# Two of four weight-block sums per feature made by accumulating transfers, and a fast product scheme rewritten with one half's rows negated

## The chip, the cores and the metric

The kernel runs on one core of a Trainium2 chip. The metric is the device time of one launch in microseconds (us), lower is better. A core has five engines that run their own instruction streams in order: TensorE (PE in the profile; its weight loads are shown apart as PEld), VectorE (DVE), ScalarE (ACT), GpSimd (POOL) and SyncE (SP). SP only issues transfers here; a transfer that SP, ACT or POOL has issued is carried out by sixteen DMA engines while the issuing engine goes on. An instruction that waits for a transfer or for another engine holds up everything behind it on its own engine.

## The reference

One layer of a hybrid encoder trunk is applied to a prompt of 2048 tokens and to a sample of 8 x 16 tokens, with model width 1024. Chunk-band attention and an mLSTM run side by side and are mixed by an out-projection. A gated convolutional feed-forward network (FFN) follows, and the change lies there:

```python
def conv_ffn(h, buf, w_up, w_conv, b_conv, w_down):
    u = h @ w_up                                   # 1024 -> 2 * 2816: gate rows, up rows
    ext = jnp.concatenate([buf.astype(u.dtype), u], axis=1)
    y = b_conv
    for j in range(CONV_W):                        # causal depthwise convolution, width 3
        y = y + ext[:, j:j + S] * w_conv[j]
    gate, up = jnp.split(y, 2, axis=-1)
    out = (jax.nn.gelu(gate, approximate=True) * up) @ w_down
    return out, ext[:, S:]
...
x = x + rms_norm(mix, norm_g[1])
ffn, new_buf = conv_ffn(rms_norm(x, norm_g[2]), conv_buf, w_up, w_conv, b_conv, w_down)
x = x + rms_norm(ffn, norm_g[3])
```

Everything is float32, and the caches, the states and the last two rows of `u` are outputs too.

## The kernel before, in words

**Stages.** The tokens are 16 prompt tiles of 128 rows and one sample tile. The kernel first makes the combined in-projection, with attention and mLSTM mixed in between its matmuls; then the out-projection with residual and norm, tile by tile; then the FFN. A float32 product is three matmuls in a faster format (`mm3`, L95 to L97): each operand is split into a rounded part "hi" and the rest "lo", and hi·hi, hi·lo and lo·hi are summed in PSUM. `split` makes hi on ACT (L1265) and lo on DVE (L1266).

**FFN.** The tokens go through the FFN in three blocks: tiles 0 to 5, tiles 6 to 11, and tiles 12 to 15 with the sample. Each block has an up phase and a down phase. The up phase runs over 22 features `f`; a feature is 128 gate rows and 128 up rows of `u`. Its 2 x 2 block product ([gate; up] by [two halves of the model width] by [two halves of the tokens]) is made by Strassen's scheme in Winograd's form with seven products, P1 to P7, instead of eight. Each product has 4 x 3 matmuls of 384 columns, 84 per feature. The sums on the token side (`t1` to `t4`) are formed once per block, before the phase, from transposed pieces (`kept`, `part`). The results are combined as they leave PSUM: `x1` on ACT, `x2` and `x3` on DVE, then `second`, which writes the second token half of `uu` (up rows) or `ug` (gate rows). `conv` follows: POOL copies a two-column halo into the tile (L1430) and out of it (L1435), ACT does the first tap and the GELU, DVE the other two taps (L1439, L1440), and DVE multiplies gate by up (L1514). The gated rows go to DRAM (`gd`). The down phase reads them back and multiplies with `w_down`.

**The weight side.** A feature's weights are four blocks of 128 x 512 floats (256 KB each), `src(0)` to `src(3)`. With a11, a12, a22, a21 for these, the scheme needs s1 = a21 + a22, s2 = s1 − a11, s3 = a11 − a21 and s4 = a12 − s2. Products P1, P6, P7, P5 take a11, s2, s3, s1 (group 0); P2, P4, P3 take a12, a22, s4 (group 1). In the first block of tiles `load_quads` has SP load the four blocks (L1277), DVE form the four sums (L1282), and SP store them to DRAM (`wsd`, L1284). The other two blocks of tiles only load what is there. All blocks of 128 x 512 ("quads") come from one pool of 11 buffers. `load_up` then splits a group into hi and lo; the split weights rotate over three sets, so that loading runs two groups ahead of the product that uses them (`ahead_of`).

**What sets the order.** A scheduler orders each engine's instructions from the program, its dependences and its own timing; the places of the buffers come from rotating pools. The first features' weights are loaded while the out-projection is still going on. In the last tiles of that stage POOL makes steps of the norms (L78, L84) and the scaling of `mx` (L1027), which then goes to DRAM (`x2d`, L1028) and comes back for the token side.

Of the kernel before, what the change touches and what calls it, by code (L numbers as in the profile page):

```python
# [12 lines left out]
AF = mybir.ActivationFunctionType  # L13
ALU = mybir.AluOpType
# [30 lines left out]
def hymba_step(ctx: ExitStack, tc: tile.TileContext, I: dict, O: dict):  # L45
    nc = tc.nc
# [985 lines left out]

    P1, P6, P7, P5, P2, P4, P3 = range(7)
# [13 lines left out]
    def quad(name):  # L1047
        return ffn.p3.tile([P, 512], F32, tag="q", name=name, bufs=11)
# [8 lines left out]
    def h2_units(b, between=(), lead=0):  # L1057
# [3 lines left out]
        def unit(halves, col, n, nm):  # L1061
# [34 lines left out]
            def piece(what):  # L1096
                return quad(f"{what}{nm}")[:, :4 * n]
# [10 lines left out]
            def kept(src, what):  # L1108
                r = piece(what)
                nc.scalar.copy(r, src)  # L1110
                return r

            pt = turn(0, 0)
# [3 lines left out]
            pt = turn(1, 0)  # L1117
# [4 lines left out]
            pt = turn(1, 1)  # L1122
            b22, t2, t3 = kept(pt, "b22"), piece("t2"), piece("t3")
# [8 lines left out]
            nc.vector.tensor_tensor(t4, pt, t2, op=ALU.subtract)  # L1132
# [137 lines left out]
    def load_quads(b, f, g):  # L1270

        src = lambda i: I["w_up"][f][:, i * 512:(i + 1) * 512]
        if b == 0 and g == 0:
            q = []
            for i in range(4):
                q.append(quad(f"wu{f}_{i}"))
                nc.sync.dma_start(q[i], src(i))  # L1277
            a11, a12, a22, a21 = q
            s1, s2, s3, s4 = [quad(f"ws{f}_{i}") for i in range(4)]
            for o, x, y, op in ((s1, a21, a22, ALU.add), (s2, s1, a11, ALU.subtract), (s3, a11, a21, ALU.subtract),  # L1280
                                (s4, a12, s2, ALU.subtract)):
                nc.vector.tensor_tensor(o, x, y, op=op)  # L1282
            for i, o in enumerate((s2, s3, s1, s4)):
                nc.sync.dma_start(wsd[f][:, i * 512:(i + 1) * 512], o)  # L1284
            raws[f] = [a12, a22, s4]
            return [a11, s2, s3, s1]
# [116 lines left out]
    for b, tiles in enumerate(FBLOCKS):  # L1403
# [13 lines left out]
        def second(u, x, acc):  # L1417

            add = lambda o, c, v=lambda t: t: nc.vector.tensor_tensor(o, v(x[:, c]), v(acc[:, c]), op=ALU.add)  # L1419
# [58 lines left out]
        for f in range(NF):  # L1478
# [12 lines left out]
            nc.vector.tensor_tensor(x2[:, :n], x1[:, :n], d_[:, :n], op=ALU.add)  # L1491
            product(P7, w[2], e)
            nc.vector.tensor_tensor(x3[:, :n], x2[:, :n], e[:, :n], op=ALU.add)
            product(P5, w[3], c)
            uu = u_tile(f"uu{nm}")
            second(uu, x3, c)
# [11 lines left out]
            nc.vector.tensor_tensor(uu[:, 2:2 + n], x2[:, :n], e[:, :n], op=ALU.add)  # L1508
            product(P3, w[2], c, onto=True)
            second(ug, x2, c)  # L1510
# [184 lines left out]
```

## Time and profile before

| what | value |
|---|---|
| time, median of 3 runs (lowest, highest) | 2793.34 us (2790.7, 2794.12) |
| the profiled execution's own time | 2786.45 us |
| its span, from first to last instruction | 2784.7 us |
| granted TensorE clock, mean | 0.998 |
| instructions | 47088 |
| bytes moved | 486.05 MB, 175 GB/s over the span |
| first block's up phase (first P1 matmul to first down matmul) | 1313.45 to 1641.75 us |

The span is what the profile can explain; the time has 1.75 us more around it. In a row of a group the columns are line, engine, operation, tiles (written <- read), shape, count, then busy time in us and mean ns of one, then the engine's idle time before these instructions and what ended it. In a row of the waits, "PE ua L97 <- DVE wul L1266: 3.0, 2, 1.6" says that matmuls of L97 into `ua` waited for DVE's L1266 writing `wul`: 3.0 us in all, 2 times, 1.6 at most. A row of a table by windows has the window, its length, busy time (and instructions) of PE, PEld, DVE, ACT and POOL, then the granted clock, the DMA engines' busy share and GB/s. A row of the timeline has start, duration, engine, line, operation, and in brackets the wait ahead of it.

### The profile page before, as it was taken

What the parts mean: (1) busy time and instruction counts of PE and PEld (TensorE: products, weight loads), DVE (VectorE), ACT (ScalarE), POOL (GpSimd) and SP (SyncE); (2) the same over time, 40 slices, a digit from 0 to 9 for tenths busy, and PEclk for the clock granted to TensorE, in tenths of its full rate; (3) what the DMA queues carried; (4) which work ended last, traced back from release to release, by engine and by line L of the source; (5) the groups of instructions that cost most, each with busy time, mean ns of one, the idle gap of its engine ahead of it and who ended that gap; (6) DMA issues with size and microseconds to landing.
All of it is one profiled execution on the core that took longest, in us unless ns stands there. A gap on an engine that the chain in (4) does not pass through costs nothing.

```text
span 2784.7 us, 47088 instructions
## 1 busy us (share of the span) xinstructions
PE 2723.8 (98%) x16587; PEld 2548.3 (92%) x16587; DVE 1876.3 (67%) x3447; ACT 1409.1 (51%) x2836; POOL 437.4 (16%) x895
## 2 busy tenths in 40 slices
PE   8999999999999999999999999999999999999998
PEld 7899999998899998888999988899999878999887
DVE  5344455656556668666999986457877864888855
ACT  4355555644356666544454555345455543555543
POOL 1000010212000003244111110011111310222220
PEclk9999999999999999999999999999999999999999
DMA  5544355557555555356655455644544774555585
GB/s 185 155 119 136 103 174 162 164 157 217 162 173 148 144 179 171 107 176 227 187 172 167 167 176 174 219 142 153 160 152 141 276 263 152 172 179 180 192 309 190
DMA packets 311883, 486.05 MB, mean 175 GB/s; under 512 B 55426, under 2 KB 150622, under 8 KB 311518
## 3 DMA queue, kind: packets, MB, share of 16 engines
q1 hardware_dynamic: 271134, 442.92, 50.1%
q10 hardware_dynamic: 38592, 33.83, 3.6%
q0 software_dynamic: 1920, 6.29, 0.6%
q8 instruction: 130, 2.13, 0.3%
q14 instruction: 107, 0.88, 0.1%
HBM read 359.36 MB, written 126.70 MB: 175 GB/s over the span
## 4 chain that ended last, share of the span: by engine, by line
PE 55%; DVE 2%; DMA 1%; issue 1%; ACT 1%; POOL 1%; SPq 0%; DVEq 0%; POOLq 0%; ACTq 0%
PE uec L95 6%; PE uec L96 6%; PE uec L97 6%; PE dn L97 4%; PE dn L96 4%; PE dn L95 4%; PE ua L97 3%; PE ua L95 3%; PE ua L96 3%; PE dnm L97 2%; PE dnm L95 2%; PE dnm L96 2%; PE wo L97 2%; PE wo L95 2%; PE wo L96 2%; PE ub L96 1%
## 5 line engine op out<-in xcount | busy, mean ns | idle before, releaser
L95 PE MATMUL uec<-B,wuh 128*128 128x384 f32 (+1 forms) x720 | 234.9, 328 | 2.2 <-DVE uu L1419 1.1
L96 PE MATMUL uec<-B,wuh 128*128 128x384 f32 (+1 forms) x720 | 235.1, 327 | 0.0
L97 PE MATMUL uec<-B,wul 128*128 128x384 f32 (+1 forms) x720 | 233.9, 327 | 0.0
L1266 DVE TENSOR_TENSOR gl<-gr,gh 128x768 fp32r<-128x768 f32 (+3 forms) x141 | 120.4, 863 | 145.8 <-ACT gh L1265 144.5
L1265 ACT CAST gh<-gr 128x768 fp32r<-128x768 f32 (+3 forms) x141 | 102.0, 735 | 200.1 <-PE dn L96 183.2
L1265 ACT CAST wuh<-wu 128x512 fp32r<-128x512 f32 x255 | 141.7, 617 | 112.1 <-PE uec L96 103.2
L95 PE MATMUL dn<-wdh,gh 128*128 128x512 f32 x466 | 182.4, 391 | 2.3 <-DVE ug L1419 2.3
L96 PE MATMUL dn<-wdl,gh 128*128 128x512 f32 x466 | 183.4, 394 | 0.0
L97 PE MATMUL dn<-wdh,gl 128*128 128x512 f32 x466 | 167.9, 396 | 0.0
L1266 DVE TENSOR_TENSOR wul<-wu,wuh 128x512 fp32r<-128x512 f32 x255 | 164.6, 683 | 2.8 <-DMA x2d<-mx 2.8
L393 DVE CUSTOM_DVE_ANT_0 tmp<-s,nb 128x640 f32<-128x640 f32 (+4 forms) x128 | 94.4, 737 | 96.6 <-PE s L383 94.8
L95 PE MATMUL vo<-wi_h,hT 128*128 128x256 f32 x544 | 155.1, 285 | 0.6 <-DVE mt L199 0.6
L97 PE MATMUL vo<-wi_h,hT 128*128 128x256 f32 x544 | 155.6, 286 | 0.0
L96 PE MATMUL vo<-wi_l,hT 128*128 128x256 f32 x544 | 154.8, 285 | 0.0
L95 PEld LDWEIGHTS uec<-B,wuh 128*128 128x128 f32 x720 | 135.0, 188 | 4.2 <-DVE uu L1419 1.6
L95 PE MATMUL qk<-hT,wi_h 128*128 128x384 f32 (+1 forms) x384 | 128.7, 335 | 7.4 <-ACT qk_st L224 6.6
L96 PEld LDWEIGHTS uec<-B,wuh 128*128 128x128 f32 x720 | 135.2, 188 | 0.2
L97 PEld LDWEIGHTS uec<-B,wul 128*128 128x128 f32 x720 | 135.1, 188 | 0.0
L406 DVE TENSOR_TENSOR ptl<-pt,pth 128x640 fp32r<-128x640 f32 (+4 forms) x128 | 93.6, 737 | 57.1 <-ACT pth L405 56.0
L394 ACT ACTIVATE tmp<-tmp,mn 128x640 f32<-128x640 f32 (+4 forms) x128 | 97.6, 762 | 64.6 <-DVE mn L393 61.9
L96 PE MATMUL qb<-hT,wi_h 128*128 128x384 f32 (+1 forms) x384 | 127.8, 333 | 0.0
L96 PE MATMUL qk<-hT,wi_h 128*128 128x384 f32 (+1 forms) x384 | 127.6, 332 | 0.0
(412 smaller groups left out, 8873.0 us busy)
## 6 DMA issues: line engine op xcount, KB each, us to landing
wu<-in_w_up SPq DMA_DIRECT2D x220, 256.0 KB, 4.1
wu<-wsd SPq DMA_DIRECT2D x176, 256.0 KB, 4.2
wdr<-in_w_down SPq DMA_DIRECT2D x132, 256.0 KB, 5.6
gr<-gd SPq DMA_DIRECT2D x78, 384.0 KB, 3.6
wi_raw<-in_w_in SPq DMA_DIRECT2D x52, 512.0 KB, 4.0
wsd<-ws SPq DMA_DIRECT2D x88, 256.0 KB, 2.8
gd<-g SPq DMA_DIRECT2D x44, 384.0 KB, 3.5
kraw<-kTd SPq DMA_DIRECT2D x112, 128.0 KB, 3.2
```

Of the source, the lines that this page charges most:

```text
L95: nc.tensor.matmul(out, ah, bh, start=start, stop=False, skip_group_check=onto)
L96: nc.tensor.matmul(out, ah, bl, start=False, stop=False, skip_group_check=onto)
L97: nc.tensor.matmul(out, al, bh, start=False, stop=stop, skip_group_check=onto)
L393: nc.vector.tensor_tensor_reduce(o_, s_, b_, 1.0, 3e38, ALU.add, ALU.min, accum_out=mn)
L394: nc.scalar.activation(tmp[:, :n], tmp[:, :n], AF.Exp, bias=mn, scale=-1.0, accum_out=rsum[:, i % 4, hh:hh + 1])
L406: nc.vector.tensor_tensor(s.ptl[:, sl, qc], ptv, s.pth[:, sl, qc], op=ALU.subtract)
L1265: nc.scalar.copy(h, r)
L1266: nc.vector.tensor_tensor(l, r, h, op=ALU.subtract)
```

## The change

The sums s1 and s3 are no longer formed by DVE. For each, SP loads the block a21 into the sum's own buffer, and POOL issues a second transfer from DRAM that adds onto it while it is written: a22 onto s1, a11 onto s3. So s1 is a21 + a22 as before, and s3 is now a21 + a11 instead of a11 − a21. The transfer can only add, so the scheme is rewritten with the gate rows' blocks taken as negated: DVE's two sums become s2 = s1 + a11 and s4 = a12 + s2, the block `b22` and the sum `t4` of the token side change sign, `x2`, `x3` and the first half of `uu` become differences, and the gate's `second` undoes the sign with a `scalar_tensor_tensor` (x times −1, minus the product) where a `tensor_tensor` stood. The layout of the weights in DRAM is as before. Per feature, in the first block of tiles, SP issues five loads instead of four, POOL issues two accumulating transfers where it had none, DVE forms two sums instead of four, and seven quad buffers are taken instead of eight.

```diff
-            def kept(src, what):
+            def kept(src, what, sign=1.0):
                 r = piece(what)
-                nc.scalar.copy(r, src)
+                nc.scalar.activation(r, src, AF.Copy, scale=sign)
                 return r
...
-            b22, t2, t3 = kept(pt, "b22"), piece("t2"), piece("t3")
+            b22, t2, t3 = kept(pt, "b22", -1.0), piece("t2"), piece("t3")
...
-            nc.vector.tensor_tensor(t4, pt, t2, op=ALU.subtract)
+            nc.vector.tensor_tensor(t4, t2, pt, op=ALU.subtract)
...
         if b == 0 and g == 0:
-            q = []
-            for i in range(4):
-                q.append(quad(f"wu{f}_{i}"))
-                nc.sync.dma_start(q[i], src(i))
-            a11, a12, a22, a21 = q
-            s1, s2, s3, s4 = [quad(f"ws{f}_{i}") for i in range(4)]
-            for o, x, y, op in ((s1, a21, a22, ALU.add), (s2, s1, a11, ALU.subtract), (s3, a11, a21, ALU.subtract),
-                                (s4, a12, s2, ALU.subtract)):
-                nc.vector.tensor_tensor(o, x, y, op=op)
+            s1, s3 = [quad(f"ws{f}_{i}") for i in (0, 2)]
+            for s_ in (s1, s3):
+                nc.sync.dma_start(s_, src(3))
+            a11, a12, a22 = [quad(f"wu{f}_{i}") for i in range(3)]
+            for i, q in enumerate((a11, a12, a22)):
+                nc.sync.dma_start(q, src(i))
+            nc.gpsimd.dma_start(s1, src(2), accum_op=ALU.add)
+            nc.gpsimd.dma_start(s3, src(0), accum_op=ALU.add)
+            s2, s4 = [quad(f"ws{f}_{i}") for i in (1, 3)]
+            for o, x, y in ((s2, s1, a11), (s4, a12, s2)):
+                nc.vector.tensor_tensor(o, x, y, op=ALU.add)
             for i, o in enumerate((s2, s3, s1, s4)):
                 nc.sync.dma_start(wsd[f][:, i * 512:(i + 1) * 512], o)
...
-            add = lambda o, c, v=lambda t: t: nc.vector.tensor_tensor(o, v(x[:, c]), v(acc[:, c]), op=ALU.add)
+            def add(o, c, v=lambda t: t):
+                if sign > 0:
+                    nc.vector.tensor_tensor(o, v(x[:, c]), v(acc[:, c]), op=ALU.add)
+                else:
+                    nc.vector.scalar_tensor_tensor(o, v(x[:, c]), -1.0, v(acc[:, c]), op0=ALU.mult, op1=ALU.subtract)
...
-            nc.vector.tensor_tensor(x2[:, :n], x1[:, :n], d_[:, :n], op=ALU.add)
+            nc.vector.tensor_tensor(x2[:, :n], d_[:, :n], x1[:, :n], op=ALU.subtract)
...
-            nc.vector.tensor_tensor(x3[:, :n], x2[:, :n], e[:, :n], op=ALU.add)
+            nc.vector.tensor_tensor(x3[:, :n], x2[:, :n], e[:, :n], op=ALU.subtract)
...
-            second(uu, x3, c)
+            second(uu, x3, c, 1.0)
...
-            nc.vector.tensor_tensor(uu[:, 2:2 + n], x2[:, :n], e[:, :n], op=ALU.add)
+            nc.vector.tensor_tensor(uu[:, 2:2 + n], x2[:, :n], e[:, :n], op=ALU.subtract)
...
-            second(ug, x2, c)
+            second(ug, x2, c, -1.0)
```

The lines of the changed kernel are a few higher than before: its loads of a21 stand at L1277, the other loads at L1280, the accumulating transfers at L1281 and L1282, the stores at L1287, the halo copies at L1438 and L1443. In the names, `ws12_0`, `_1`, `_2`, `_3` are s1, s2, s3, s4 of feature 12, `wu12_0` to `_2` its blocks a11, a12, a22 (and before also `_3`, a21), and `wsd` is the sums' place in DRAM.

On SP, in the middle of the first block's up phase, before the change (features 11 and 12):

```order
L1284 DMA wsd11_281<-ws11_0_17797 128x512
L1284 DMA wsd11_281<-ws11_1_17798 128x512
L1519 DMA gd0_7_211<-g0_7_17476 128x768
L1284 DMA wsd11_281<-ws11_2_17799 128x512
L1277 DMA wu12_0_17944<-in_w_up 128x512
L1284 DMA wsd11_281<-ws11_3_17800 128x512
L1277 DMA wu12_1_17946<-in_w_up 128x512
L1277 DMA wu12_2_17948<-in_w_up 128x512
L1277 DMA wu12_3_17950<-in_w_up 128x512
```

On SP at the same place after the change:

```order
L1287 DMA wsd11_281<-ws11_1_17801 128x512
L1277 DMA ws12_0_17944<-in_w_up 128x512
L1287 DMA wsd11_281<-ws11_3_17802 128x512
L1277 DMA ws12_2_17945<-in_w_up 128x512
L1280 DMA wu12_0_17948<-in_w_up 128x512
L1280 DMA wu12_1_17949<-in_w_up 128x512
L1287 DMA wsd12_282<-ws12_0_17944 128x512
L1280 DMA wu12_2_17950<-in_w_up 128x512
L1527 DMA gd0_8_212<-g0_8_17629 128x768
L1287 DMA wsd12_282<-ws12_2_17945 128x512
L1287 DMA wsd12_282<-ws12_1_17956 128x512
L1277 DMA ws13_0_18099<-in_w_up 128x512
```

The loads of a21 for feature 12 stand right behind the stores of s2 and s4 of feature 11, and the stores of feature 12's s1 and s3, which POOL's transfers finish, stand ahead of the load for feature 13.

On POOL, near the end of the out-projection, after the change (before, the rows marked DMA were not there and the others stood in this order):

```order
L1281 DMA ws0_0_16184<-in_w_up 128x512
L1027 TENSOR_TENSOR mx13_15920<-mx13_15920 128x1024
L1282 DMA ws0_2_16185<-in_w_up 128x512
L78 TENSOR_SCALAR wssq14_0_16061<-wssq14_0_16061 128x1
L1281 DMA ws1_0_16247<-in_w_up 128x512
L78 TENSOR_SCALAR n1_14_ms_16104<-wssq14_1_16101,wssq14_0_16061 128x1
L84 TENSOR_TENSOR n1_14_rs_16106<-n1_14_ms_16104,nhalf_74 128x1
L1027 TENSOR_TENSOR mx14_16034<-mx14_16034 128x1024
L1282 DMA ws1_2_16248<-in_w_up 128x512
```

The transfers of features 0 and 1 stand in POOL's queue between the norm steps of tiles 13 and 14.

On POOL in the middle of the up phase, after the change (before, only the copies were there):

```order
L1438 COPY ug0_9_17731<-halo_15181 128x2
L1443 COPY halo_15181<-uu0_9_17721 128x2
L1281 DMA ws12_0_17944<-in_w_up 128x512
L1438 COPY uu0_10_17874<-halo_15181 128x2
L1282 DMA ws12_2_17945<-in_w_up 128x512
L1438 COPY ug0_10_17886<-halo_15181 128x2
```

Each accumulating transfer now stands behind a halo copy, and the next halo copies behind it.

More of the change, by code (lines that the diff above doesn't have):

```diff
@@ L1415, in product, with second @@
                     start=not onto and k == 0, stop=k == 3, onto=onto)
-        def second(u, x, acc):
-            add = lambda o, c, v=lambda t: t: nc.vector.tensor_tensor(o, v(x[:, c]), v(acc[:, c]), op=ALU.add)
+        def second(u, x, acc, sign):
+            def add(o, c, v=lambda t: t):
[3 more added lines that the diff above has]
+                    nc.vector.scalar_tensor_tensor(o, v(x[:, c]), -1.0, v(acc[:, c]), op0=ALU.mult, op1=ALU.subtract)
             if not last:
```

## Prediction

> **What bounds the kernel now.** First the page's busy times, then the table by windows around the first block's up phase, the only place where weights are loaded in the new way.
>
> ```profile
> PE 2723.8 (98%) x16587; PEld 2548.3 (92%) x16587; DVE 1876.3 (67%) x3447; ACT 1409.1 (51%) x2836; POOL 437.4 (16%) x895
> ...
> 1300.00:1320.00 20.00, 20.00 (x97) 17.34 (x96) 12.55 (x18) 10.11 (x19) 6.34 (x8) 1.00 0.89 315
> 1320.00:1630.00 310.00, 304.00 (x1725) 300.74 (x1724) 286.31 (x434) 157.89 (x251) 58.59 (x82) 0.99 0.53 174
> 1320.00:1340.00 20.00, 17.85 (x100) 16.96 (x99) 20.00 (x25) 9.62 (x13) 3.79 (x3) 1.00 0.58 194
> ```
>
> PE is busy 98% of the span and 304.0 of 310 us in this phase, so PE's work sets the end. DVE is close behind here: 286.31 of 310, 92%, and all of the first 20 us. The waits from 1300 to 1640 us say what PE's gaps are, and what DVE itself waits for:
>
> ```profile
> PE ua L97 <- DVE wul L1266: 3.0, 2, 1.6
> PE uec L95 <- DVE uu L1419: 1.1, 1, 1.1
> PE uec L95 <- DVE ug L1419: 1.0, 1, 1.0
> PE ub L97 <- DVE wu L1266: 0.6, 1, 0.6
> PE uec L95 <- DVE x L1493: 0.3, 1, 0.3
> PE uec L95 <- DVE uu L1508: 0.2, 1, 0.2
> ...
> DVE ws L1282 <- DMA wu<-in_w_up: 12.4, 13, 3.8
> ```
>
> PE loses 3.0 + 1.1 + 1.0 + 0.6 + 0.3 + 0.2 = 6.2 us to a late DVE. That is all that relieving DVE can return here. It is 0.22% of the run, and 0.2% (5.6 us) is about what a measurement of this kernel can tell from no change. In the timeline the phase reaches from its first P1 matmul to the first down matmul:
>
> ```profile
> 1313.45 0.34 PE L95 MATMUL ua<-B,wuh 128*128 128x384 f32 x1
> ...
> 1641.75 0.50 PE L95 MATMUL dnm<-wdh,gh 128*128 128x512 f32 x1 [0.53 <-ACT wdh L1265]
> ```
>
> So 328.3 us for 22 features, 14.92 each; without the 6.2 it is 14.64. I work with 14.6 as the period below which anything else hides.
>
> **The change: DVE's relief.** DVE's groups in the phase:
>
> ```profile
> L1282 DVE TENSOR_TENSOR ws<-wu,wu 128x512 f32<-128x512 f32 x40 | 27.5, 686 | 12.4 <-DMA wu<-in_w_up 12.4
> L1439 DVE SCALAR_TENSOR_TENSOR y<-uu,wcv,y 128x768 f32<-128x768 f32 x20 | 20.2, 1012 | 1.5 <-issue 1.5
> L1514 DVE TENSOR_TENSOR g<-y,y 128x768 f32<-128x768 f32 x19 | 18.1, 952 | 0.9 <-ACT y L1442 0.9
> L1419 DVE TENSOR_TENSOR ug<-x,uec 128x384 f32<-128x384 f32 x20 | 11.0, 548 | 4.1 <-PE uec L97 4.0
> ```
>
> Two sums go per feature: 44 x 0.686 = 30.2 us of DVE, which falls from about 92% to 83% of the phase. This lies beside PE; only the 6.2 can come back, and not all of it, because part of it starts from late weights rather than a full DVE:
>
> ```profile
> 1385.78 0.69 DVE L1282 TENSOR_TENSOR ws<-wu,wu 128x512 f32<-128x512 f32 x1 [3.80 <-DMA wu<-in_w_up]
> ...
> 1387.08 0.42 PE L95 MATMUL uec<-B,wuh 128*128 128x384 f32 x1 [0.96 <-DVE ug L1419]
> 1389.06 0.69 PE L97 MATMUL ua<-B,wul 128*128 128x384 f32 x1 [1.39 <-DVE wul L1266]
> ```
>
> DVE stood 3.80 us for a load, and 0.96 + 1.39 of PE's wait follow. A load still precedes s2, with another transfer behind it, so I count little of that 2.35 and most of the other 3.85: 2.8 us back (bounds 0 and 6.2).
>
> **The signs.** The differences in place of sums are the same instruction. The gate's `second` becomes a three-operand form. The trace has that form only on 768 columns, 1012 ns against 952 for the two-operand one: +0.06 each. The 110 of them (22 in each of the first two blocks, 66 smaller ones in the last) make 6.6 us of DVE, hidden by PE except where PE waits for the last feature of a phase: three times, 0.2 us. If a product read from PSUM costs more in that form, by the whole 0.55 of L1419, it is 0.55 x 3 = 1.7 on the path. Negating b22 is in nine ACT copies that exist already: nothing, as ACT is 51% busy; without that cover 9 x 0.6 = 5 us.
>
> **The price of a transfer.** No accumulating transfer is in the trace. Its nearest rows are POOL's own plain transfers of the same 256 KB, and SP's loads of the weights:
>
> ```profile
> L1378 POOL DMA_DIRECT2D out_y_prompt<-f x24: 557/557/760, 2181.2 to 2680.2; - x24
> DMA to landing us min/median/max: 2.3/5.5/7.4
> ...
> L1277 SPq DMA_DIRECT2D wu<-in_w_up x76: 327/382/1006, 1340.2 to 1605.3; - x76
> DMA to landing us min/median/max: 3.3/4.9/5.9
> ...
> wu<-in_w_up SPq DMA_DIRECT2D x220, 256.0 KB, 4.1
> ```
>
> (The first landing row is POOL's stores, the second SP's loads in the phase.) I call the time from POOL's issue to landing X. The median store is 5.5; an accumulation also reads what it adds to, 256 KB more, and at the 315 GB/s that 0.89 of the DMA engines moved at 1300 us, thus 354 in full, that is 0.7. So X = 6.2, with bounds 2.3 and 7.4 + 0.7 = 8.1. For a load L I take 4.4, between the whole run's 4.1 and the phase's 4.9, since a21 no longer stands behind three sisters.
>
> The Trainium skill's "DMA: Bandwidth & Descriptors" (Anatomy of one DMA — SWDGE path) fits a GpSimd-issued transfer with 2.0 us plus its bytes at 436 GB/s, an estimated 2.6 us here. The trace's median of 5.5 speaks against it under this load; with 2.6 the sum below would be 5.6 us under the time before.
>
> More reads also load the DMA engines: 3 x 22 x 262 KB = 17.3 MB in 328 us is 53 GB/s on 174, and 0.53 busy becomes about 0.7. Not a bound.
>
> **The start.** The first features' sums are made while PE finishes the out-projection:
>
> ```profile
> 1291.57 0.62 SPq L1277 DMA_DIRECT2D wu<-in_w_up  x1
> ...
> 1301.01 1.22 DVE L199 TENSOR_TENSOR mt<-mT_pt,mt 128x1024 fp32r<-128x1024 f32 x1
> 1302.72 0.39 PE L97 MATMUL wo<-wo,mt 128*128 128x512 f32 x1
> ...
> 1304.07 0.27 POOL L78 TENSOR_SCALAR n_ms<-wssq,wssq 128x1 f32<-128x1 f32 x1 [4.86 <-ACT mt L1016]
> 1306.37 2.40 POOL L1027 TENSOR_TENSOR mx<-mx 128x1024 f32<-128x1024 f32 x1 [1.40 <-DVE mx L1026]
> 1311.55 0.69 DVE L1266 TENSOR_TENSOR wul<-wu,wuh 128x512 fp32r<-128x512 f32 x1 [2.81 <-DMA x2d<-mx]
> 1314.50 0.34 PE L97 MATMUL ua<-B,wul 128*128 128x384 f32 x1
> ```
>
> Chain one: a21 lands at 1291.57 + 4.1, a22 is on it X later, then DVE makes s2 and s4 (1.37) and `mt`'s lo (1.22), which PE needs at 1302.72. It is there at 1298.3 + X: PE waits X − 4.5. Chain two: the load of a21 for feature 1 is queued on SP behind the stores of feature 0's sums, and its accumulation on POOL ahead of tile 14's norm. So that norm starts no sooner than 1295.7 + X + 0.69 (s2) + 0.8 (two SP issues) + 4.4 (load) = 1301.6 + X. As before, 1306.37 − 1304.07 = 2.3 us later `mx` is scaled (2.40), and 1311.55 − 1308.77 = 2.8 us after that DVE splits the first weights, ready at 1309.8 + X where PE wants them at 1314.50: X − 4.7. The two overlap. Some of it comes back: in the next 20 us PE had 2.15 idle behind a full DVE, which now has four sums fewer; I count 1.1. The start costs X − 5.6: +0.6 at 6.2, −3.3 at 2.3 and +2.5 at 8.1.
>
> **The loop in the middle.** The new order ties one feature's load to the last one's transfer. On SP, the load of s3's a21 stands behind the store of the previous s4, and the next feature's first load behind the stores of s3 and s2. Over two features the circle is: DVE from s2 to s4 (0.68 + 1.01 + 0.61 + two weight splits of 0.68 + 0.68, as DVE's order has it, 4.35), five SP issues (5 x 0.382 = 1.9), two loads and two accumulations: 6.25 + 2(L + X). It hides while under 29.2, thus while L + X is under 11.5. I have 4.4 + 6.2 = 10.6: hidden, with 0.9 us spare. POOL's halo copies stand among the transfers too; POOL was busy 58.59 of 310 us, so it has room.
>
> **Sum.** −2.8 (relief) + 0.2 (signs) + 0.6 (start) + 0 (loop) = −2.0. On the profiled execution's 2786.45 that gives 2784.4; its median of three runs is 6.9 higher, 2793.34, so I say **2791**. This case alone reaches from 2787 (X = 2.3, −5.9) to 2796 (X = 8.1 and no relief, +2.7).
>
> **Rivals.**
>
> *The loop becomes the bound (slower).* It decides at L + X = 11.5. With L at the phase's 4.9 and X at 7.4 (the longest POOL store), a feature takes 3.1 + 12.3 = 15.4, 0.8 over PE's; over the 18 features that don't live on the start's lead, 14, plus 1.8 at the start, 0.2 for signs: +16, **2809**. With the largest of both, 5.9 + 8.1, it is 2.5 x 18 + 2.7 = +48, 2841. For: 0.9 spare out of 10.6 on a price that no row shows. Against: only if the order keeps all five steps in line does the circle close. 32%.
>
> *POOL's issue is starved by DVE (slower).* Small POOL instructions can take far longer than their work in this phase:
>
> ```profile
> L1435 POOL COPY halo<-uu 128x2 f32<-128x2 f32 x21 | 23.1, 1100 | 51.8 <-DVE uu L1419 51.8
> ...
> L1435 POOL COPY halo<-uu x66: 179/514/3254, 1333.2 to 2615.3; 128x2 f32<-128x2 f32 x66
> ```
>
> A copy of two columns takes 0.18 us at its best, 1.10 on the mean here and up to 3.25. If writing the transfer's descriptors suffers alike, X grows by 0.9 to 3.1, to 7.1 to 9.3, and the loop binds from L + X = 11.5 on: at L = 4.4, 0 to 2.2 per feature, +2 to +45; the middle, +20, is **2813**. The Trainium skill's "SBUF — State Buffer" (SBUF: two separate sides) names such a mechanism, POOL kept from writing descriptors while DVE holds a shared port. By its words only DVE's two-port modes do that to the descriptors; no run here tells yet. 13%.
>
> *All of DVE's lateness goes (faster).* If X is near its lowest and the 6.2 vanish whole, with the start no worse, it is 6.2 − 0.2 = −6.0, **2787.3**. For: DVE loses 10% of its work. Against: 2.35 of the 6.2 comes from a load. 13%.
>
> **How the numbers follow.** The hidden loop has 42%, the binding loop 32%, starvation 13%, full relief 13%. Same, between 2787.8 and 2798.9, is the first case: 0.42. Faster is the last: 0.13. Slower, the two others: 0.45. The range runs from 2786 to 2815: it leaves out the far ends of the binding loop (a third of it, 11%) and half of the starvation (6%).
>
> **What would show it.** Right: DVE's busy time in the up phase of the first block falls by 30 us, PE's stays over 98%, the phase stays within 328 ± 3, and POOL's transfers land in under 7 us. The binding loop: PE and DVE wait for an accumulating transfer in the same place every feature, some 15.4 us apart, and SP's stores wait for POOL's transfers. Starvation: the same with long issues on POOL. If the phase of the first block isn't changed but the other two blocks are, the signs have a price that I hold to be nil, and the prediction fails for that reason.

## The result, and the profile after

| | before | after |
|---|---|---|
| time, median of 4 runs each | 2793.73 us | 2818.21 us |
| ratio of after to before, 95% interval | | 1.0081 (1.0056 to 1.0105) |
| the profiled execution: span, mean granted clock | 2784.7 us, 0.998 | 2817.1 us, 0.994 |

The change makes the kernel 0.81% slower. The ratio is one of means, and by it the loss is 22.6 us; the medians differ by 24.5. The forecast was no measurable change, and the measured time lies 3 us above the range.

The page and the windows of the profile after (columns as before), then the up phase of the first block as one window, from its first P1 matmul to the first down matmul, before and after:

```profile
PE 2735.9 (97%) x16587; PEld 2556.7 (91%) x16587; DVE 1849.2 (66%) x3403; ACT 1407.9 (50%) x2836; POOL 457.8 (16%) x939
...
1300.00:1320.00 20.00, 18.41 (x83) 14.62 (x82) 6.41 (x9) 6.33 (x14) 8.06 (x10) 1.00 0.87 232
1320.00:1340.00 20.00, 16.58 (x79) 15.33 (x78) 12.51 (x16) 9.23 (x16) 10.28 (x10) 0.91 0.86 274
1320.00:1630.00 310.00, 293.38 (x1635) 287.16 (x1634) 253.22 (x374) 150.21 (x240) 78.63 (x121) 0.99 0.82 226
...
1313.45:1641.75 328.30, 321.77 (x1825) 318.19 (x1823) 302.85 (x457) 168.46 (x268) 61.92 (x88) 0.99 0.54 178
...
1324.68:1669.95 345.27, 326.22 (x1825) 319.75 (x1823) 281.17 (x416) 167.72 (x268) 81.10 (x131) 0.99 0.78 219
```

DVE has its relief (286.3 to 253.2 us busy), but PE fell from 304.0 to 293.4 in the same 310 us, and the DMA engines went from 0.53 busy to 0.82. The phase has the same 1825 matmuls in both and is 17.0 us longer: PE stands idle for 19.1 us where it was 6.5, and the matmuls themselves keep it busy 4.5 us longer. The spans differ by 32.4 us, more than the medians. The last group of the in-projection, in the profile before and after, shows why:

```profile
L97 PE MATMUL vo<-wi_h,hT x544: 274/281/384, 252.1 to 1044.3; 128*128 128x256 f32 x182
...
L97 PE MATMUL vo<-wi_h,hT x544: 274/281/420, 253.8 to 1054.2; 128*128 128x256 f32 x182
```

It ends at 1044.3 and at 1054.2 us, and up to there both kernels have the same instructions in the same order on every engine. In the profiles of the experiments that leave this part alone it ends between 1044.3 and 1055.8 us. So 9.9 us of the 32.4 are put down to these two executions and not to the change; 22.5 are left, close to the 22.6 of the ratio. I take 9.9 off below. Where the rest arises is read from the copies of P1's product (`x1`) for features 0, 3, 6 and 18 and the first down matmul, before and then after:

```profile
1316.43 0.48 ACT L1489 COPY x<-ua 128x384 f32<-128x384 f32 x1 [0.42 <-PE ua L97]
1358.99 0.48 ACT L1489 COPY x<-ua 128x384 f32<-128x384 f32 x1 [0.52 <-PE ua L97]
1407.03 0.48 ACT L1489 COPY x<-ua 128x384 f32<-128x384 f32 x1
1586.83 0.48 ACT L1489 COPY x<-ua 128x384 f32<-128x384 f32 x1 [1.20 <-PE ua L97]
...
1332.84 0.47 ACT L1497 COPY x<-ua 128x384 f32<-128x384 f32 x1
1375.03 0.48 ACT L1497 COPY x<-ua 128x384 f32<-128x384 f32 x1 [0.60 <-PE ua L97]
1428.50 0.48 ACT L1497 COPY x<-ua 128x384 f32<-128x384 f32 x1
1610.70 0.48 ACT L1497 COPY x<-ua 128x384 f32<-128x384 f32 x1
...
1669.95 0.50 PE L95 MATMUL dnm<-wdh,gh 128*128 128x512 f32 x1 [0.53 <-ACT wdh L1266]
```

The changed kernel is late by 16.4 − 9.9 = 6.5 us at feature 0, 6.1 at feature 3, 11.6 at feature 6, 14.0 at feature 18, and 28.2 − 9.9 = 18.3 at the down phase. So 6.5 us are lost at the start, 5.5 between features 3 and 6, and 6.7 from there to the end of the phase. A value at one feature is rough, since from feature 3 on the kernel before has its features 10 to 19 us apart. Another 4.2 follow after the phase; the kernel with the signs alone (`e1_signs` below, ratio 0.9998) has 2.7 there too, so they can't be told from one execution's noise.

The waits after, from 1300 to 1680 us:

```profile
PE uec L95 <- DVE x L1501: 7.5, 6, 2.5
PE ua L97 <- DVE wul L1267: 5.8, 3, 3.4
PE ua L95 <- ACT wuh L1266: 2.5, 4, 0.7
PE uec L95 <- DVE uu L1424: 2.2, 2, 1.8
PE wo L97 <- DVE mt L199: 1.6, 1, 1.6
...
DVE ws L1285 <- DMA ws<-in_w_up: 35.8, 11, 5.2
```

These five waits of PE make 19.6 us, 17.1 of them for DVE, where its waits for DVE made 6.2 before. The largest, for `x3` at L1501, was 0.3. DVE itself now stands 35.8 us at s2 (L1285) for the accumulating transfer. The start in the timeline: SP's load of a21, POOL's addition, s2 on DVE, the same for feature 1, tile 14's scaling on POOL, and what PE waited for:

```profile
1300.95 0.63 SPq L1277 DMA_DIRECT2D ws<-in_w_up  x1
1305.95 1.09 POOL L1281 DMA_DIRECT2D ws<-in_w_up  x1 [1.92 <-DMA lated<-t]
1311.23 0.69 DVE L1285 TENSOR_TENSOR ws<-ws,wu 128x512 f32<-128x512 f32 x1 [5.19 <-DMA ws<-in_w_up]
1312.89 0.75 SPq L1277 DMA_DIRECT2D ws<-in_w_up  x1
1319.14 0.88 POOL L1281 DMA_DIRECT2D ws<-in_w_up  x1 [8.56 <-DMA ws<-in_w_up]
1322.39 2.41 POOL L1027 TENSOR_TENSOR mx<-mx 128x1024 f32<-128x1024 f32 x1 [1.40 <-DVE mx L1026]
1328.56 0.69 DVE L1267 TENSOR_TENSOR wul<-wu,wuh 128x512 fp32r<-128x512 f32 x1 [5.66 <-DMA x2d<-mx]
1329.31 0.44 PE L97 MATMUL ua<-B,wul 128*128 128x384 f32 x1 [3.42 <-DVE wul L1267]
```

At 1329.31 PE has stood 3.42 us for the first weights. After that its matmuls are slow for a while:

```profile
1330.00:1335.00 5.00, 5.00 (x22) 5.00 (x21) 5.00 (x9) 4.22 (x9) 2.40 (x1) 0.66 0.86 243
```

The granted clock of these 5 us is 0.66. From that first lo matmul to the end of P1's product it takes 3.0 us, where it took 1.9 before, so about 1.1 of the 6.5 us at feature 0 are a slower PE and not a wait.

And the step between features 3 and 6, with the eviction behind s2 and PE's waits (POOL's and DVE's rows as above):

```profile
1367.40 0.90 SPq L1277 DMA_DIRECT2D ws<-in_w_up  x2
1373.36 0.84 POOL L1281 DMA_DIRECT2D ws<-in_w_up  x1 [5.57 <-DMA ws<-in_w_up]
1380.40 0.69 DVE L1285 TENSOR_TENSOR ws<-ws,wu 128x512 f32<-128x512 f32 x1 [4.79 <-DMA ws<-in_w_up]
1382.67 0.91 SPq L1277 DMA_DIRECT2D ws<-in_w_up  x2
1386.47 0.84 POOL L1281 DMA_DIRECT2D ws<-in_w_up  x1 [2.60 <-DMA ws<-in_w_up]
1393.37 0.69 DVE L1285 TENSOR_TENSOR ws<-ws,wu 128x512 f32<-128x512 f32 x1 [4.50 <-DMA ws<-in_w_up]
...
1394.90 0.55 DVE L1424 TENSOR_TENSOR uu<-x,uec 128x384 f32<-128x384 f32 x1
...
1381.75 0.45 PE L97 MATMUL ua<-B,wul 128*128 128x384 f32 x1 [0.84 <-DVE wul L1267]
1386.28 0.45 PE L95 MATMUL uec<-B,wuh 128*128 128x384 f32 x1 [1.00 <-DVE x L1501]
1395.51 0.44 PE L95 MATMUL uec<-B,wuh 128*128 128x384 f32 x1 [1.79 <-DVE uu L1424]
```

From load to s2 it is 13.0 us, then 10.7. DVE stands 4.79 and 4.50 for it, with splits and evictions behind s2 in its queue, and PE waits for these: at 1395.51 for the eviction that DVE made 1.5 us after s2. The longest wait of this step comes with feature 6's weights, whose s2 stands directly ahead of the eviction `x3` (the view names no releaser for DVE's 1.71 us; POOL issued the addition onto s1 at 1400.85, and it landed 5.4 us later):

```profile
1406.28 0.69 DVE L1285 TENSOR_TENSOR ws<-ws,wu 128x512 f32<-128x512 f32 x1 [1.71 <-issue]
1406.89 0.55 DVE L1501 TENSOR_TENSOR x<-x,uec 128x384 f32<-128x384 f32 x1
1407.49 0.45 PE L95 MATMUL uec<-B,wu 128*128 128x384 f32 x1 [2.50 <-DVE x L1501]
```

This place comes back every third feature. For the weights of features 6, 9, 12, 15, 18 and 21 the order on DVE has s2 directly ahead of `x3`, an eviction of an earlier feature; DVE stands 1.7 to 4.1 us for s1 there, and PE then waits 2.50, 1.65, 0, 0.47, 0.69 and 1.17 us for `x3`. For features 8, 11, 14, 17 and 20 s2 stands two or three instructions ahead of the next eviction; DVE stands 0.4 to 2.9 us, and PE doesn't wait. For the features between, s1 is there when DVE comes to s2.

### The profile page after: what moved, and what is told of

Same layout as the page of the kernel before. It is cut to its first block, busy times and chain, and to the rows that moved or that the text cites. A ratio compares the mean times of both kernels' runs of the same rounds, so it can differ in the third digit from the quotient of the medians.

```text
span 2817.1 us, 47241 instructions
## 1 busy us (share of the span) xinstructions
PE 2735.9 (97%) x16587; PEld 2556.7 (91%) x16587; DVE 1849.2 (66%) x3403; ACT 1407.9 (50%) x2836; POOL 457.8 (16%) x939
## 4 chain that ended last, share of the span: by engine, by line
PE 52%; DMA 4%; DVE 2%; issue 1%; ACT 1%; POOL 1%; DVEq 0%; SPq 0%; POOLq 0%; ACTq 0%
PE uec L95 5%; PE uec L96 5%; PE uec L97 5%; PE dn L97 4%; PE dn L96 4%; PE dn L95 4%; PE ua L95 3%; PE ua L97 3%; PE ua L96 3%; PE dnm L97 2%; PE dnm L95 2%; PE dnm L96 2%; DMA ws<-in_w_up 2%; PE wo L95 2%; PE wo L97 2%; PE wo L96 2%
## 5 line engine op out<-in xcount | busy, mean ns | idle before, releaser
L97 PE MATMUL qk<-hT,wi_l 128*128 128x384 f32 (+1 forms) x384 | 128.1, 334 | 0.0
```

Of the source, the lines that this page charges most:

```text
L97: nc.tensor.matmul(out, al, bh, start=False, stop=stop, skip_group_check=onto)
```

## The experiments

Ratios are to the kernel before on the same chip, with 95% intervals.

**1. Which part of the change costs.** First the signs alone (`e1_signs`):

```diff
-            (s1, s3 by accumulating transfers)
+            for o, x, y in ((s1, a21, a22), (s2, s1, a11), (s3, a21, a11), (s4, a12, s2)):
+                nc.vector.tensor_tensor(o, x, y, op=ALU.add)
```

> The changed kernel with the sums s1 = a21 + a22 and s3 = a21 + a11 made by DVE again from four loads (no accumulating transfer); the new signs stay. Theory (the two transfers in series that s1 and s3 now need are what costs): the signs are free, within 0.2% of the kernel before, 2789 to 2799 us. Rival (the signs cost, by the gate's three-operand form reading PSUM or by the token side): 2803 us or more.

Measured: 2789.08 us, ratio 0.9998 (0.9989 to 1.0007). The signs cost nothing that shows; the loss is in the transfers.

Then the relief without the additions (`e3_no_add`), and POOL's transfers overwriting instead of adding (`e4_plain`):

```diff
-            nc.gpsimd.dma_start(s1, src(2), accum_op=ALU.add)
-            nc.gpsimd.dma_start(s3, src(0), accum_op=ALU.add)
```

> The changed kernel without the accumulating transfers: SP loads a21 into the buffers of s1 and s3 and nothing is added to them, so both sums are left out. DVE's relief and the fifth load stay, the series of two transfers and POOL's part are gone. Theory (two transfers in series): back at the kernel before or under it by the relief, 2787 to 2794 us. Rival (more traffic makes all loads late): five loads of the seven are left, so a third to a half of the loss stays, 2802 us or more.

Measured: 2785.63 us, 0.9991 (0.9982 to 1.0000). DVE's relief, with the fifth load included, is worth 2.5 us; the interval reaches from 0 to 5.

```diff
-            nc.gpsimd.dma_start(s1, src(2), accum_op=ALU.add)
+            nc.gpsimd.dma_start(s1, src(2))
```

> The changed kernel with POOL's two transfers per feature overwriting instead of adding (the sums s1 and s3 are left out; order, queues and waits as changed). Theory (the series of two transfers): as the changed kernel, 2812 to 2820 us. Rival (the addition itself is what is slow, since it also reads what it adds to): landing falls from 5.0 to about 4.3 us or less, and the time by 8 us or more, to 2810 us or under.

Measured: 2795.47 us, 1.0023 (1.0014 to 1.0032). The rival's line holds: the time falls under 2810 us and the landing to 3.8 us. Two plain transfers in series do cost, but only 6.5 us of the 22.6. The other 16 need the addition. The issue on POOL in the whole phase, then the landing and the queue's share of the DMA engines from 1340 to 1640 us, for the changed kernel and then for the plain transfers:

```profile
L1281 POOL DMA_DIRECT2D ws<-in_w_up x22: 838/847/1086, 1306.0 to 1631.1; - x22
ws<-in_w_up POOLq DMA_DIRECT2D x40, 256.0 KB, 5.0
q0 software_dynamic: 5760, 10.49, 21.5%
...
L1281 POOL DMA_DIRECT2D ws<-in_w_up x22: 536/536/761, 1298.3 to 1605.7; - x22
ws<-in_w_up POOLq DMA_DIRECT2D x38, 256.0 KB, 3.8
q0 software_dynamic: 3153, 10.32, 10.9%
```

An addition's issue takes 0.31 us longer, it lands 1.2 us later (counted from the start of its issue), and it holds the DMA engines twice as long for the same bytes.

One POOL transfer alone, plain and with no load in front (`e11_pool_first`):

```diff
-            for s_ in (s1, s3):
-                nc.sync.dma_start(s_, src(3))
...
-            nc.gpsimd.dma_start(s1, src(2), accum_op=ALU.add)
+            nc.gpsimd.dma_start(s1, src(2))
```

> The changed kernel with s1 and s3 loaded by POOL alone, a plain transfer of a22 and of a11 and no load of a21 in front (the sums are left out): one transfer on POOL in place of two in series, all waits behind them kept. Theory (L + X in series is what closes the circle; here only X, 3.8 + 0.5 us): 2784 to 2791 us. Rival (any transfer by POOL that SP and DVE wait for costs): as with the plain overwrite, 2794 us or more.

Measured: 2789.59 us, 0.9999 (0.9990 to 1.0007). POOL's queue as such costs nothing that shows. From the start of the first issue to the landing of the data in s1's buffer the four kernels have 3.7 us (no addition), 3.9 (one POOL transfer), and, as medians over the features in the traces, 9.1 (two plain) and 10.2 (the change); they stand at −2.5, −0.3, +6.5 and +22.6 us. At 3.9 it hides, at 9.1 it no longer does, and the last 1.1 us, with the heavier load of the additions, cost more than the 5.2 before them. DVE has the same instructions in the same order with two plain transfers; at the six places ahead of `x3` it stands 0.3 to 2.0 us there, against 1.7 to 4.1.

**2. Where in the phase.** DVE makes the sums of the first six (`e2_from6`) or two features (`e18_from2`), accumulating transfers follow:

```diff
+            if f < 6:      # or 2
+                (loads and sums as in e1_signs)
+            else:
                 (as changed)
```

> The changed kernel with DVE making s1 and s3 for the features 0 to 5, and accumulating transfers only from feature 6 on. Theory that the start is what costs (the profile shows the phase 11.5 us late by feature 6, beyond what it was before the phase): 2804 to 2808 us. Rival that every feature pays alike (16 of 22 features keep the transfers): 2811 us or more. If the loop is never bound once the start is over, and the phase's last features aren't late either: 2794 us.

> Accumulating transfers from feature 2 on; the sums of features 0 and 1, made while the out-projection ends, by DVE. The changed kernel is 0.81% slower, the one from feature 6 on 0.28%. If the loss of the first six features is a lead lost at the start (6 us at feature 0, 7.5 us at feature 4): as from feature 6 on, 2794 to 2799 us. If each of the first features pays for itself while the transfers are crowded: 2801 us or more.

Measured: 2797.28 us, 1.0028 (1.0018 to 1.0038), which meets none of its three lines, and 2804.9 us, 1.0057 (1.0043 to 1.0072). The first six features carry two thirds of the loss; of the first two it is 0.24 of 0.81, with intervals that overlap. So it is not one lead lost at the start: with the start mended, the step behind it still comes. In the trace of `e18_from2` feature 6's copy follows feature 3's by 1413.17 − 1360.60 = 52.6 us, where the kernel before has 48.0.

**3. The load on the DMA engines, or the wait.** The additions beside a kernel that doesn't need them (`e7_traffic`):

```diff
+            for k, i in enumerate((2, 0)):
+                nc.gpsimd.dma_start(scr[f][:, k * 512:(k + 1) * 512], src(i), accum_op=ALU.add)
```

> The new signs with all sums by DVE, and beside them the same two accumulating transfers per feature into scratch in DRAM that nobody reads: the additions' load on POOL and on the DMA engines without any wait for them. Rival (the DMA engines' time for additions costs by itself): 2795 us or more. Theory (only the wait for them costs): under 2792 us.

Measured: 2847.95 us, 1.0210 (1.0196 to 1.0224), but the loss lies elsewhere. Since they wait for nothing, the transfers were issued at the kernel's beginning:

```profile
L97 PE MATMUL vo<-wi_h,hT x544: 274/281/384, 306.2 to 1100.6; 128*128 128x256 f32 x182
```

This group starts 54 us late (252.1 before); the phase itself, 1371.5 to 1698.9 us, is as long as before. A second kernel ties them to the gated rows of each feature (`e10_traffic_in_place`):

```diff
             nc.sync.dma_start(gd[b][f][:, :nt * P], gt[:, :nt * P])
+            if b == 0:
+                for k in range(2):
+                    nc.gpsimd.dma_start(scr[f][:, k * 512:(k + 1) * 512],
+                                        gd[b][f][:, k * 256:k * 256 + 512], accum_op=ALU.add)
```

> The new signs, all sums by DVE, and per feature two accumulating transfers of 256 KB on POOL's queue from the just stored gated rows to scratch in DRAM, which nobody reads: the additions' load in its place, without a wait for it on DVE or SP. Circle through SP: within 0.15% of the kernel before, 2785 to 2793 us. Rival (the load on the DMA engines): 2797 us or more.

Measured: 2794.84 us, 1.0018 (1.0009 to 1.0026): 5 us (2.5 to 7), between the two lines. So additions by their load alone (into DRAM here, not SBUF) may cost about a quarter of the loss; by this run the rest is the wait. In the profile the load doesn't lengthen the phase: with the DMA engines 0.73 busy it takes 327.2 us, against 326.0 with the signs alone and 328.3 in the kernel before. Where the 5 us arise isn't shown.

One addition per feature, s3 only, s1 by DVE from landed blocks (`e8_s3_only`):

```diff
+            s3 = quad(f"ws{f}_2")
+            nc.sync.dma_start(s3, src(3))
...
+            nc.gpsimd.dma_start(s3, src(0), accum_op=ALU.add)
...
+            for o, x, y in ((s1, a21, a22), (s2, s1, a11), (s4, a12, s2)):
```

> Only s3 is made by an accumulating transfer (22 instead of 44), s1 by DVE from four loads; s3 is needed by no further sum, so DVE never waits for POOL. Theory (what costs is the late s1, behind which DVE's sums and splits and then PE wait): 2785 to 2792 us. Rival (each addition costs its share): half of the loss, 2797 to 2802 us.

Measured: 2811.44 us, 1.0074 (1.0061 to 1.0087): nearly the whole loss with half the additions and no sum that waits for one. Both lines fall. Its waits from 1314 us on, of DVE and SP:

```profile
DVE ws L1283 <- DMA wu<-in_w_up: 27.3, 13, 6.6
...
SPq L1285 <- DMA ws<-in_w_up: 118.4, 20, 7.5
```

SP's store of s3 stood 118.4 us for the addition, and DVE stood 27.3 us (12.4 before) at its sums for plain loads. So DVE need not wait for an addition itself to stand still; that the stores on SP make these loads late fits, but wasn't tried apart.

**4. Where the circle closes.** POOL's halo copies taken off its queue (`e6_halo_act`):

```diff
-            nc.gpsimd.tensor_copy(u[:, 0:2], halo[:, ct, :])
+            (nc.scalar.copy if b == 0 else nc.gpsimd.tensor_copy)(u[:, 0:2], halo[:, ct, :])
```

> The changed kernel with the halo copies of the first block made by ACT instead of POOL, so that no accumulating transfer stands behind a copy that waits for DVE (POOL's copies waited 61.1 + 18.6 us for y in the phase). Theory that POOL's queue is part of the circle: 2803 us or less. If the circle runs through SP and the transfers alone: 2807 to 2815 us. ACT gets 88 copies more, under 20 us of its time, hidden.

Measured: 2812.15 us, 1.0073 (1.0059 to 1.0087). POOL's halo copies are not it.

The stores of s1 and s3 moved from SP to ACT (`e5_act_stores`):

```diff
-                nc.sync.dma_start(wsd[f][:, i * 512:(i + 1) * 512], o)
+                (nc.scalar if i in (1, 2) else nc.sync).dma_start(wsd[f][:, i * 512:(i + 1) * 512], o)
```

> The changed kernel with the stores of s1 and s3, which wait for POOL's transfers, issued by ACT instead of SP; nothing else. Times against 2788 us for the kernel before and 2811 us for the changed one on that scale. Theory (a circle through SP: the next load stands behind a store that waits for the addition): at least half of the loss goes, 2800 us or less. Rival (the additions hold the DMA engines, whatever the order): 2807 to 2815 us. If ACT's waits for the transfers hold up the splits and the evictions: over 2815 us.

Measured: 2859.39 us, 1.0260 (1.0238 to 1.0281): ACT, which makes the hi parts, evicts and feeds the convolution, now stands for the transfers, 102.7 us in three groups of its waits. It leaves SP's part open. Three kernels give SP's stores another source, `e9_store_other`, `e14_store_old` and `e16_store_a11`:

```diff
-            for i, o in enumerate((s2, s3, s1, s4)):
+            for i, o in enumerate((a12, a11, a22, a12)):                # e9
...
+                old = hist[-2][1][0].bitcast(F32) if len(hist) > 1 else a11   # e14: the last feature's s2, hi
+                old = hist[-2][0][0].bitcast(F32) if len(hist) > 1 else a11   # e16: the last feature's a11, hi
```

> The changed kernel, but SP's four stores per feature write blocks that were only loaded (a12, a11, a22, a12) in place of the sums, so that no store on SP waits for an addition or for a sum of DVE (the second and third blocks then multiply with other weights). Transfers, bytes and additions are as many. Times against 2789 us for the kernel before and 2811 us for the changed one on that scale. Theory (a circle through SP's queue: load, addition, store that waits for it, next load): the loss is gone or nearly, 2794 us or less. Rival (the additions hold the DMA engines and make all transfers late): 2803 us or more.

> The changed kernel with SP's four stores per feature reading an already split block of the previous feature instead of the sums (the second and third blocks then multiply with other weights): as many bytes and transfers, and no store that waits for a load, an addition or a sum. The run before this one of that kind had its stores wait for the loads instead, 142 us against 148. Theory (SP's in-order waits close the circle): 2795 us or less. Rival (buffers and DVE's order, SP not needed): 2803 us or more.

> The changed kernel with SP's four stores per feature reading the already split block a11 of the previous feature, which no addition and no sum touches (the second and third blocks then multiply with other weights). The earlier run of this kind read a block that was itself split from s2, so SP still waited for the chain, one feature behind. The trace of the changed kernel shows a circle in the first features: s2 on DVE, its store on SP, the next load of a21 behind it (2.3 to 4.8 us after s2), the addition (5 us later), the next s2 (5 to 7 us later). Theory (this circle through SP's queue): the loss goes to 2796 us or less (kernel before 2788, changed 2811). Rival (buffers and DVE's order): 2803 us or more.

Measured: 2817.92 us, 1.0097 (1.0082 to 1.0112); 2813.24, 1.0085 (1.0069 to 1.0100); 2809.07, 1.0067 (1.0052 to 1.0081). The first two don't take the wait off SP: the stores then waited for loads (142 us), and for a part split from s2. In the third no store waits for an addition or a sum, and at most a small part of the loss goes. But SP isn't free there either: its stores stand 68.2 us for the hi part of a11 on ACT (165.6 us for additions and sums in the changed kernel, both from 1300 to 1680 us), and its loads of a21 stand 64.6 us for splits on DVE that free a buffer (26.8 in the changed kernel). DVE's waits at s2 in the third kernel, from 1314 us on:

```profile
DVE ws L1285 <- issue: 14.9, 6, 4.6
DVE ws L1285 <- DMA ws<-in_w_up: 13.7, 5, 5.8
```

It still stands 28.6 us (the profile finds no releaser for half of them), against 35.3 in the changed kernel. So SP's wait for the additions is not what closes the circle, or not alone.

A twelfth quad buffer in the changed kernel (`e12_quads12`), in the kernel before (`e13_before_quads12`), from feature 6 on (`e15_from6_q12`), and with the stores of `e16_store_a11` (`e17_store_a11_q12`):

```diff
-        return ffn.p3.tile([P, 512], F32, tag="q", name=name, bufs=11)
+        return ffn.p3.tile([P, 512], F32, tag="q", name=name, bufs=12)
```

> The changed kernel with 12 instead of 11 quad buffers (room from a scratch row kept in bfloat16 and split tiles cut to the 1024 columns in use). Times against 2789 us for the kernel before and 2811 us for the changed one. Theory of the buffers (a load of a21 can only be issued when DVE's split of the previous weights frees a buffer, and from there load and addition are too long for the place of s2 in DVE's order): one buffer more lets loads go earlier, and at least half of the loss goes, 2800 us or less. Rival (SP's wait for the additions): 2806 us or more.

> The kernel before with the same 12 quad buffers: what the extra buffer is worth there. It had 12.4 us of DVE waiting for loads, of which 2.4 us reached PE: 2784 to 2790 us by either theory. It is the reference for the run with 12 buffers.

> Accumulating transfers from feature 6 on, and 12 quad buffers. If buffers are the limit, the +0.28% of the run with 11 buffers is gone: 2785 to 2791 us, as the kernel before with 12 buffers or up to 2 us under it by DVE's relief. If not: 2795 us or more.

> The same with 12 quad buffers: neither SP's stores nor the eleventh buffer hold a load. If SP and buffers together close the circle: 2793 us or less, under the run with 11 buffers. If DVE's order does (s2 stands in DVE's queue ahead of the evictions at a place where the two transfers in series are not done yet, wherever the load starts): 2803 us or more.

Measured: 2822.12 us, 1.0119 (1.0104 to 1.0134); 2790.13, 1.0004 (0.9995 to 1.0012); 2802.04, 1.0049 (1.0034 to 1.0065); 2824.52, 1.0122 (1.0106 to 1.0138). A buffer more makes the kernels with additions slower by 0.2 to 0.6%, and leaves the kernel before where it was. The timelines of DVE and PE in `e12_quads12` show what goes on:

```profile
1541.60 0.69 DVE L1285 TENSOR_TENSOR ws<-ws,wu 128x512 f32<-128x512 f32 x1 [3.86 <-DMA ws<-in_w_up]
1542.21 0.55 DVE L1516 TENSOR_TENSOR uu<-x,uec 128x384 f32<-128x384 f32 x1
...
1542.81 0.69 PE L95 MATMUL uec<-B,wuh 128*128 128x384 f32 x1 [2.52 <-DVE uu L1516]
```

The scheduler now puts s2 ahead of the eviction at L1516, one eviction earlier than in the changed kernel (L1501). DVE stands 3.86 us for the addition with that eviction behind it, and PE waits 2.52 for its accumulator. It is the same link as at 1407.49 us above. For the same six features (6, 9, ..., 21) DVE stands 20.3 us here and 16.1 in the changed kernel, and PE waits 15.0 us for the eviction behind s2 here and 6.5 there: PE loses time because a sum that isn't ready stands ahead of an eviction in DVE's queue, and the more the earlier PE needs that eviction. The lower clock adds to it: over the phase the granted clock is 0.96, and the 1825 matmuls keep PE busy 331.5 us against 326.2.

## Why the prediction was wrong

**Right: what could be won, and the signs.** The relief was put at 2.8 us of at most 6.2; it is 2.5 (0 to 5), so it is borne out in size only within these bounds. The signs were put at 0.2 us; they cost nothing that shows.

**Right: the size of a hop, nearly.** L + X was put at 4.4 + 6.2 = 10.6. Over the phase the medians to landing, counted from the start of the issue as the working does, are 4.5 and 5.1 to 5.3, together 9.7; with the time until POOL comes to issue it is 10.2 from load to sum. So X was put 0.9 us too high. The page weighed there (the Trainium skill's "DMA: Bandwidth & Descriptors", Anatomy of one DMA — SWDGE path) would have had an estimated 2.6 us for X. A plain POOL transfer lands in 3.7 to 4.5 here and an accumulating one, in the changed kernel, in 5.0 to 5.3, so the trace's row was the better guide. For starvation of POOL's issue nothing speaks: the issues took 0.84 to 1.09 us at L1281 and 0.85 to 1.45 at L1282.

**Mis-sized: the load on the DMA engines.** Their traffic was put at 174 + 53 = 227 GB/s and came out at 226, but they are 0.82 busy and not 0.7. The additions hold them twice as long for their bytes as plain transfers do (21.5% against 10.9%).

**Wrong: the start, X − 5.6 = 0.6.** From the first load's issue to PE's first lo matmul it was 1314.50 − 1291.57 = 22.9 us before and 1329.31 − 1300.95 = 28.4 after, 5.5 more. The working's first chain came true: s2 starts 10.3 us after the first load, as in 4.1 + X, though by a longer load (5.0 to POOL's addition) and a shorter X (5.3), and PE's wait for `mt` is 1.6 us where X − 4.5 gives 1.7. The second chain failed. Its path is the one named (load, addition, store, load for feature 1, addition ahead of tile 14's norm, `mx`, `x2d`, split), but 1309.8 + X − 1291.57 gives 24.4 us and not 28.4. The load for feature 1 to POOL's addition took 6.25 (4.4 in the working), from there to `mx` 3.25 (2.3, without the addition's own issue of 0.88 on POOL), `mx` to the split 3.75 (2.8). So it doesn't lie under the first chain's wait: PE stands another 3.42 us, and P1 takes 1.1 us more at the lower clock behind it, a term that the working doesn't have. Nor did the 1.1 us counted as coming back do so: PE's two waits in the next 20 us are 0.36 and 1.53, together 1.9, where it had 2.15. At feature 0 the kernel is 6.5 us late.

**Wrong: the loop, 0.** "It hides while L + X is under 11.5" compares a mean time with a mean period. (The terms named for DVE's part add up to 3.66 and not 4.35, which would make the limit 11.8.) By that test the loop hides with room, since L + X is 9.7; yet DVE stood 35.8 us at s2 for additions, and 12.2 us are lost from feature 3 to the end of the phase, where the working had 0. What counts is whether s1 has landed when DVE comes to the place that s2 has in its order, and which eviction stands behind it. The hop of 13.0 us (5.96 to POOL's issue, 7.04 to s2) and the next one go through to PE between features 3 and 6; after that it is the place ahead of `x3`, every third feature. A term for these waits isn't in the sum. The circle named in the working, through the stores on SP, isn't shown to be the one that counts: with stores that wait for no addition 0.67% of 0.81% stay, though SP stood for other things there. The rival "the loop becomes the bound" had the right sign, and 2809 us. Its signs came half true: SP's stores wait for POOL's transfers (150.3 us, 43 times), and the waits do come back in the same place, but every third feature, some 46 us apart, and at 6.7 us over the last 16 features they cost half of the 0.8 us per feature that it counted.

**What is shown, and what stays open.** Shown: the transfers cost it all; the loss grows with the time from load to data; in the traces PE's waits come from a DVE that stands at s2 ahead of an eviction, and with s2 one eviction further ahead they more than double. Most of the loss is this wait; the load on the DMA engines, beyond what it adds to the landing times, has about 5 us of it (2.5 to 7), and a lower clock after long waits some. Open: what makes the data late once the lead is gone. Taking POOL's halo copies away, giving SP's stores another source and a twelfth buffer didn't bring the time back, but in the second of these SP still stood for splits and for buffers, so SP's queue isn't ruled out. That DVE's order decides is read from the traces and from a kernel whose order changed together with its buffers; a kernel with s2 held back behind the evictions, and nothing else changed, wasn't tried. No version with accumulating transfers beat the kernel before.

## What to carry to other kernels

Work moved from a busy engine to transfers is free only while the data still come before the place that the order gives to their first reader, and a load followed by an accumulating transfer took 10.2 us here where a load alone took 4.5. A cover that is judged by means (10.6 under 11.5) fails where the pipeline starts and wherever the order puts the reader early; ask what the lead is at the start, and what stands behind the waiting instruction. Where PE already has 98%, such a relief can bring only the few us that PE waits for that engine, while every us of lateness there counts in full.

## What the runs showed of the hardware

An accumulating transfer of 256 KB from DRAM to SBUF lands in 5.0 us (median from 1340 to 1640 us; 4.3 to 7.0 over the phase) against 3.8 for a plain one on the same queue, and its queue takes 21.5% of the DMA engines' time for 10.49 MB against 10.9% for 10.32 MB, with 5760 packets against 3153.

The granted clock of the profiled executions was 0.998 in the kernel before, and 0.990, 0.991 and 0.989 in the slowest kernels of the study (ratios 1.012, 1.021 and 1.026). It is low right after long waits of PE: 0.91 in the window of 1320 to 1340 us above, where PE stood 3.42 us, and 0.91 again from 1400 to 1420 us, where it stood 2.50. In the traces it falls to 0.5 for some 3.4 us. From 1290 to 1720 us, over all twenty profiles, this follows within 6 us on 42 of the 48 waits of PE that last 2 us or more, and on 12 of the 218 that last 0.3 to 2 us. So behind a long wait PE mostly loses some 1.7 us more (an estimate: half of 3.4); whether the wait is the cause wasn't tried.

Identical instructions up to 1045 us took up to 10 us longer in one execution than in another, so a span from one profile can't settle half a per cent.
